# Keys and values of the memory: two heads to a pass, 512 columns wide, in two accumulators

## The chip, the cores and the metric

The kernel runs on one core of one Trainium2 chip. The time is the device time of one execution in microseconds (us). The program has five engines: TensorE (PE in the profile; its weight loads are PEld), VectorE (DVE), ScalarE (ACT), GpSimd (POOL) and SyncE (SP), which issues most transfers.

## What is computed

One layer of a streaming encoder on 512 tokens of width 1024: a mixer of three head groups (causal pooling, an RWKV-7 recurrence in chunks of 64 tokens, differential attention), a cross-attention of 4 heads into 256 memory tokens, and a gated MLP. The change concerns the keys and values of the memory:

```python
def memory_cross_attention(xn, memn, wq, wk, wv, wo, q_norm, k_norm):
    q = rms_normalize((xn @ wq).reshape(B, S, XA_HEADS, XA_HEAD)) * q_norm
    k = rms_normalize((memn @ wk).reshape(B, M, XA_HEADS, XA_HEAD)) * k_norm
    v = (memn @ wv).reshape(B, M, XA_HEADS, XA_HEAD)
    s = jnp.einsum('bshd,bmhd->bhsm', q, k) * (XA_HEAD ** -0.5)
    p = jax.nn.softmax(s, axis=-1)
    o = jnp.einsum('bhsm,bmhd->bshd', p, v).reshape(B, S, D_MODEL)
    return o @ wo
```

M is 256, XA_HEADS is 4, XA_HEAD is 256, and `wk` and `wv` are 1024 x 1024.

## The kernel before

Every large product is made of three matmuls (`mm3`, lines 331 to 333): each operand is split into a high and a low part, and high x high, high x low and low x high are added up in one accumulator. The helper has the same three lines for all products, so in the profile they are told apart by tiles and shapes. Weights come in units of 128 x 1024 values, each loaded in two halves of 512 columns. For each half SyncE issues a transfer, ScalarE makes the high part (`wh`, line 174) and VectorE the low part (`wl`, line 175). Five halves of each part have room.

The memory's keys and values depend on the memory alone. They are made while the mixer runs: `k_rows(h)` and `v_rows(h)` for the four heads are the eight "K" steps of the string `MIX`, in which each letter stands for a piece of work and which gives the order in which the pieces are recorded. A scheduler then orders the instructions of each engine. It may move work up to where its operands and buffers are ready, and it uses the K matmuls, which wait for nothing but weights, between pieces that wait.

One K step (`mgroup`, lines 995 to 1007) takes the 256 weight columns of one head. It makes 16 products (8 blocks of the contraction by 2 blocks of memory rows), that is 48 matmuls with 256 streaming columns. Both row blocks share one bank of PSUM, tag `a0`, which has one buffer; the last step uses a bank of tag `pd`. For K, ScalarE copies the bank out (line 1014). The step "k" (`k_norm`) sums squares, takes a power on GpSimd (line 1023) and scales on VectorE (line 1026). The step "e" (`k_t`) transposes on TensorE into a bank of tag `a0` (line 1034), and ScalarE copies that out (line 1037). The tags `a0`, `a1` and `b` also serve the large products of the mixer and of the output projection ("w"), and `pr` (two buffers) the recurrence and the scores of differential head 0.

Around the K steps stand these pieces. "t", "y" and "u" finish the inverse of the recurrence (`TX` line 805, `Y` line 814, `U` line 823). "a" makes `AT` (line 840). "c" is a chunk of the recurrence: `U` (line 905), a sum on VectorE (line 907), the state matmul `S` (line 916), and two more on VectorE (lines 923 and 924), from which the next chunk's `U` starts. "s", "o", "n" and "q" are the scores (`S`, lines 331 to 333, and VectorE's line 750), the outputs (`pT` line 775, `o`), the norm (`ss` line 788) and the transposes (`qkT` line 726) of differential attention. `k_norm` needs the rstd of the memory (line 402), which stands on GpSimd's queue behind four powers for the second pair of differential heads (line 680).

Of the kernel before, what the change touches and what calls it, by code (L numbers as in the profile page):

```python
# [10 lines left out]
F32 = mybir.dt.float32  # L11
F32R = mybir.dt.float32r
AF = mybir.ActivationFunctionType
# [3 lines left out]
P = 128  # L17
# [3 lines left out]
M = 256  # L21
# [50 lines left out]
def _pack(inputs):  # L72
    I = {k: np.asarray(v) for k, v in inputs.items()}
    f = {k: v[0] for k, v in I.items()}
    cols = []
    for n, w in _PCOLS:
        cols.append(f[n].reshape(w, P).T)
    pvec = np.concatenate(cols, 1)
    z64 = np.zeros((64, 64), np.float32)
    pw = f["pool_w"]  # L80
    pool = [np.block([[pw[2 * i], z64], [z64, pw[2 * i + 1]]]) for i in range(2)]
    wa2 = np.concatenate([f["rwkv_w2"], f["rwkv_a2"]], 0)
    lqk = np.concatenate([f["diff_lq1"], f["diff_lk1"], f["diff_lq2"], f["diff_lk2"]])
    pmat = np.concatenate(pool + [wa2, f["rwkv_g2"], np.tile(lqk[None], (P, 1))], 1)

    def fgroup(w, c0, ko):
        g = w[:, c0:c0 + 256].reshape(-1, P, 256)[list(ko)].transpose(1, 0, 2)
        return [g[:, 0:4].reshape(P, 1024), g[:, 4:8].reshape(P, 1024)]

    def tgroup(w):  # L90
        g = w.reshape(-1, P, 512).transpose(1, 0, 2)
        return [g[:, 2 * i:2 * i + 2].reshape(P, 1024) for i in range(g.shape[1] // 2)]

    def fpair(w, c0, c1, ko):
        a, b = fgroup(w, c0, ko), fgroup(w, c1, ko)
        return [a[0], b[0], a[1], b[1]]

    std = tuple(range(8))
    u = []
    wi = f["w_in"]  # L100
    for c0 in (1024, 256, 512, 768):
        u += fgroup(wi, c0, std)
    qk = [np.concatenate([wi[:, 1280 + c:1536 + c], wi[:, 1792 + c:2048 + c]], 1) for c in (0, 256)]
    one = lambda us: [[x] for x in us]
    kv = [fgroup(f[w], c0, std) for w in ("xa_wk", "xa_wv") for c0 in range(0, 1024, 256)]
    mix = {"A": one(tgroup(qk[0])), "V": one(tgroup(wi[:, 2304:2816])), "B": one(tgroup(qk[1])),
           "z": one(fgroup(wi, 0, std)),
           "K": kv,
           "w": one(fpair(f["w_out"], 0, 256, std) + fpair(f["w_out"], 512, 768, std))}
    for name in MIX:  # L110
        if name in mix:
            u += mix[name].pop(0)
    for w, ko in ((f["xa_wq"], std), (f["xa_wo"], std)):
        u += fpair(w, 0, 256, ko) + fpair(w, 512, 768, ko)
    for g in range(11):
        u += fpair(f["ffn_w_up"], g * 256, FF + g * 256, std)

    wd = f["ffn_w_down"].reshape(NF // 2, 2, P, 2, 512)
    wdown = np.stack([wd[:, 0, :, 0], wd[:, 0, :, 1], wd[:, 1, :, 1], wd[:, 1, :, 0]], 1)
    wpack = np.stack(u, 0)  # L120
    cst, bias = _consts()
    return {
        "xt": np.ascontiguousarray(I["x"][0].T),
        "memt": np.ascontiguousarray(I["mem"][0].T),
        "wp": np.ascontiguousarray(wpack),
        "wd": np.ascontiguousarray(wdown),
        "pvec": np.ascontiguousarray(pvec),
        "pmat": np.ascontiguousarray(pmat),
        "cst": cst,
        "bias": bias,  # L130
    }
# [15 lines left out]

MIX = ("iiiAAiiAAiiViVVVtjztqsyuzsjsyjsoajcBBoamconBpucjpmmBucmuccqKssccsgKsqkkososoKseogKkfsq1Ken"  # L150
       "ossoKfsKxensofooxfxxfk2fnefxwxfxwKwwwxwww1H2QQQQRSQST1RT2STSQQQRSOTOSTORO21TOSOTSTXOOXXXXX"
       "XXN")


# [39 lines left out]
def trunk_body(ctx: ExitStack, tc: tile.TileContext, A):  # L194
# [37 lines left out]
    def kvs(dt=F32, shape=(P, 512)):  # L232
        return slot("kv", TB["kv"], shape, dt)
# [10 lines left out]
    def pr(nm=None):  # L244
        return ps("pr", nm)

    def pd(nm=None):
        return ps("pd", nm)
# [517 lines left out]
    def diff_o(h, pair, keys):  # L766

        if h not in po:
            po[h] = pd("o") if h == 0 else ps("a1", "o") if h == 1 else pr("o")
        pt, m, cols = pd("pT"), 0, []  # L770
        for b in keys:
            qs = [i for i in pair if i >= b]
            cols.append((b, m, qs[0] * P, len(qs) * P))
            for i in qs:
                PE.transpose(pt[:, m:m + P], sc0[h, i][:, b * P:(b + 1) * P], ident)  # L775
                m += P
        ph, pl = pslot(), pslot()
        split(pt[:, 0:m], ph[:, 0:m], pl[:, 0:m])
        hs = slice(h * P, (h + 1) * P)
        for b, c, q0, n in cols:  # L780
            mm3(po[h][:, q0:q0 + n], vd[b][0][:, hs], vd[b][1][:, hs], ph[:, c:c + n], pl[:, c:c + n],
                b == 0, b == pair[1])
# [209 lines left out]
        ACT.activation(u, pt, AF.Copy, scale=pcol("pool_scale", i))  # L992
        ypl.append(u)

    def mgroup(tag="a0"):

        pt = ps(tag)
        for u in range(2):
            w = W.get(M)
            for j in range(4):  # L1000
                for t in range(2):
                    k = 4 * u + j
                    ah, al = mn[k]
                    sl = slice(t * P, (t + 1) * P)
                    mm3(pt[:, t * M:(t + 1) * M], ah[:, sl], al[:, sl], w[j][0], w[j][1],
                        k == 0 and t == 0, k == 7 and t == 1)
        return pt.rearrange("p (t m) -> p t m", t=2)

    KTr, Vr, kr = [], [], {}

    def k_rows(h):
        pt = mgroup()
        kr[h] = kvs(F32, (P, 2, M))
        ACT.activation(kr[h], pt, AF.Copy)

    def k_norm(h):
        k, kq = kr[h], kvs(F32, (P, 2, M))
        ss, r = small("kss", (P, 2)), small("kr", (P, 2))
        for t in range(2):
            ACT.activation(kq[:, t], k[:, t], AF.Square, accum_out=ss[:, t:t + 1])  # L1020
        V.tensor_tensor(ss, ss, rsm, ALU.mult)
        V.tensor_scalar(ss, ss, EPS, None, ALU.add)
        G.tensor_tensor(r, ss, mhalf[:, 0:2], ALU.pow)
        V.tensor_tensor(r, r, rm[0], ALU.mult)
        for t in range(2):
            V.tensor_scalar(k[:, t], k[:, t], r[:, t:t + 1], None, ALU.mult)

    def k_t(h):
        k = kr.pop(h)
        pt = ps("a0", "kT")  # L1030
        p4 = pt.rearrange("p (j m) -> p j m", j=2)
        for t in range(2):
            for j in range(2):
                PE.transpose(p4[:, j, t * P:(t + 1) * P], k[:, t, j * P:(j + 1) * P], ident)
        kt = xl(F32, (P, 2, M))
        for j in range(2):
            ACT.activation(kt[:, j], p4[:, j], AF.Copy, scale=pcol("xa_k_norm", j))
        KTr.append(kt)

    def v_rows(h):  # L1040
        pt = mgroup("pd" if h == H - 1 else "a0")
        v = xl(F32, (P, 2, M))
        for t in range(2):
            ACT.activation(v[:, t], pt[:, t], AF.Copy, scale=rm[0][:, t:t + 1])
        Vr.append(v)


    steps = {
# [427 lines left out]
```

## Time and profile before

| | us |
|---|---|
| median of 3 runs | 799.62 |
| lowest, highest | 798.34, 800.51 |
| the profiled execution's own time | 798.25 |
| its span, first to last instruction | 796.5 |
| TensorE busy in it | 785.5 |
| VectorE busy | 560.3 |
| ScalarE busy | 421.4 |

The rows are read as follows. Times count from the span's start. A matmul's row shows its whole length, in which the next one overlaps it; what TensorE pays for one is the distance to the next row's start. The granted clock is a share of 2.4 GHz, so 0.50 is 1.2 GHz. Where an engine stood idle, the row shows in brackets for how long and what ended it.

### The profile page before, as it was taken

The page shows a single profiled execution, that of the slowest core. Times are in us where ns is not written, and L with a number is a line of the kernel's source. Part 1 is how long each engine was busy: PE and PEld are TensorE (multiplying, and loading weights), DVE is VectorE, ACT ScalarE, POOL GpSimd, SP SyncE. Part 2 cuts the span into 40 slices and gives each one's busy share as a digit, 9 for nine tenths or more (in the row PEclk, how much of TensorE's full clock was granted, in tenths as well). Part 3 has the DMA queues.
Part 4 walks back from the last instruction along what each step waited for, and adds up shares of the span by engine and source line. Part 5 has one row for each costly group of instructions (what it writes and reads, how often), then busy time and mean ns, then how long its engine had stood idle before and what let it go on. Part 6 is the DMA issues. An engine that isn't in the chain of part 4 may idle for free.

```text
span 796.5 us, 11547 instructions
## 1 busy us (share of the span) xinstructions
PE 785.5 (99%) x4130; PEld 653.0 (82%) x4130; DVE 560.3 (70%) x1075; ACT 421.4 (53%) x778; POOL 64.2 (8%) x83
## 2 busy tenths in 40 slices
PE   9999999989899999999999999999999999999997
PEld 6867788879798888888888888888888888888886
DVE  7668668856898845656646577666666667898995
ACT  7464553575689854456545344433434344454662
POOL 4010400243500000000100000000000000000000
PEclk9999999979999999999999999999999999999999
DMA  7412114222031153221112322222232323534432
GB/s 278 135 56 95 64 54 133 88 74 91 16 107 55 69 168 135 94 93 54 40 66 80 133 92 93 92 94 92 93 105 81 106 94 133 176 114 133 132 93 79
DMA packets 43625, 79.22 MB, mean 99 GB/s; under 512 B 4784, under 2 KB 5936, under 8 KB 43568
## 3 DMA queue, kind: packets, MB, share of 16 engines
q1 hardware_dynamic: 41328, 75.35, 28.1%
q10 hardware_dynamic: 2240, 3.15, 1.2%
q8 instruction: 32, 0.52, 0.3%
q14 instruction: 25, 0.20, 0.1%
HBM read 76.38 MB, written 2.10 MB: 99 GB/s over the span
## 4 chain that ended last, share of the span: by engine, by line
PE 95%; ACT 1%; POOL 1%; DVE 1%; issue 1%; DMA 0%; DVEq 0%; SPq 0%; ACTq 0%
PE ps L331 23%; PE ps L333 22%; PE ps L332 22%; PE ps L1406 13%; POOL s_r L680 1%; PE T L575 1%; PE tr L523 1%; PE S L331 1%; PE colsum L393 1%; PE S L332 1%; PE S L333 1%; PE pT L775 1%; PE Sx L331 1%; PE W L608 1%; PE Sx L333 0%
## 5 line engine op out<-in xcount | busy, mean ns | idle before, releaser
L174 ACT ACTIVATE wh<-wr 128x512 fp32r<-128x512 f32 x212 | 132.5, 629 | 157.9 <-PE ps L332 119.7
L175 DVE TENSOR_TENSOR wl<-wr,wh 128x512 fp32r<-128x512 f32 x212 | 145.9, 690 | 99.5 <-ACT wh L174 95.2
L331 PE MATMUL ps<-r,wh 128*128 128x512 f32 x416 | 162.3, 394 | 0.0
L332 PE MATMUL ps<-r,wh 128*128 128x512 f32 x416 | 162.0, 389 | 0.0
L333 PE MATMUL ps<-r,wl 128*128 128x512 f32 x416 | 161.2, 390 | 0.0
L331 PEld LDWEIGHTS ps<-r,wh 128*128 128x128 f32 x416 | 78.1, 188 | 16.4 <-issue 0.2
L332 PEld LDWEIGHTS ps<-r,wh 128*128 128x128 f32 x416 | 78.1, 188 | 16.3 <-DVE t L762 0.2
L333 PEld LDWEIGHTS ps<-r,wl 128*128 128x128 f32 x416 | 78.1, 188 | 16.3
L1406 PE MATMUL ps<-whid,ma 128*128 128x512 f32 x276 | 85.2, 389 | 0.0
L331 PE MATMUL ps<-wh,xh 128*128 128x256 f32 (+1 forms) x224 | 75.3, 336 | 0.1
L332 PE MATMUL ps<-wl,xh 128*128 128x256 f32 (+1 forms) x224 | 74.8, 334 | 0.0
L1406 PEld LDWEIGHTS ps<-whid,ma 128*128 128x128 f32 x276 | 51.7, 188 | 11.2 <-ACT whid L312 0.5
L1406 PE MATMUL ps<-wlod,ma 128*128 128x512 f32 x138 | 53.4, 389 | 0.0
L312 ACT ACTIVATE whid<-r 128x512 fp32r<-128x512 f32 x55 | 34.4, 631 | 30.1 <-PE ps L1406 20.1
L1353 DVE TENSOR_TENSOR t<-ps,rb 128x512 f32<-128x512 f32 x44 | 29.4, 687 | 27.4 <-PE ps L333 27.0
L331 PEld LDWEIGHTS ps<-wh,xh 128*128 128x128 f32 x224 | 42.4, 189 | 5.4 <-issue 0.7
L332 PEld LDWEIGHTS ps<-wl,xh 128*128 128x128 f32 x224 | 42.4, 189 | 4.5 <-issue 0.7
L332 PE MATMUL ps<-xl,wh 128*128 128x512 f32 x112 | 44.0, 396 | 0.0
L313 DVE TENSOR_TENSOR wlod<-r,whid 128x512 fp32r<-128x512 f32 x55 | 37.2, 693 | 4.7 <-ACT whid L312 4.5
L332 PE MATMUL ps<-d,wh 128*128 128x512 f32 x96 | 37.7, 392 | 0.0
L333 PE MATMUL ps<-wh,xl 128*128 128x512 f32 x96 | 37.6, 393 | 0.0
L333 PE MATMUL ps<-d,wl 128*128 128x512 f32 x96 | 37.5, 390 | 0.0
(343 smaller groups left out, 1471.6 us busy)
## 6 DMA issues: line engine op xcount, KB each, us to landing
wr<-in_wp_dram SPq DMA_DIRECT2D x212, 256.0 KB, 2.6
r<-in_wd_dram SPq DMA_DIRECT2D x33, 256.0 KB, 2.8
wrawd<-in_wd_dram SPq DMA_DIRECT2D x22, 256.0 KB, 2.6
r<-in_xt_dram SPq DMA_DIRECT2D x8, 256.0 KB, 4.6
t<-in_xt_dram ACTq DMA_DIRECT2D x8, 256.0 KB, 2.7
out_dram<-t SPq DMA_DIRECT2D x8, 256.0 KB, 2.0
kv<-in_memt_dram ACTq DMA_DIRECT2D x4, 256.0 KB, 4.6
pm<-in_pmat_dram SPq DMA_DIRECT2D x1, 512.0 KB, 4.7
```

The source lines that it names most:

```text
L174: nc.scalar.activation(hi, raw, AF.Copy)
L175: nc.vector.tensor_tensor(lo, raw, hi.bitcast(F32), ALU.subtract)
L312: ins = ACT.activation(dhi, src, AF.Copy)
L313: V.tensor_tensor(dlo, src, dhi.bitcast(F32), ALU.subtract)
L331: mm(out, lh, rh, start=start, stop=False)
L332: mm(out, lh, rl, start=False, stop=False)
L333: mm(out, ll, rh, start=False, stop=stop)
L393: mm(pt[:, 2 * i:2 * i + 2], tot[:, i * P:(i + 1) * P], ones[:, 0:2], start=True, stop=True)
L523: PE.transpose(pv4[0:n, c, p, :], src(p, 2 * q + c), ident)
L575: mm(pts[hh].rearrange("p (c h t) -> p c h t", c=2, h=2)[:, c, p], KB[p][o:o + 64, cg, :], RA[p][o:o + 64, cg, :], start=True, stop=True)
L1353: V.tensor_tensor(dst[c], src[c], rb2, ALU.mult)
L1406: mm(X[p][tt], l, r, start=not onto and k == 0 and j == 0, stop=k == NG - 1 and j == 2, skip_group_check=onto)
```

## The change

A K step now takes half of the contraction for two heads at a time: 512 weight columns, two row blocks, each row block in a bank of its own (`a0` and `a1`; for the last pair of V two banks of `pd`). Two steps make one pair of heads, so the two banks are held from the first step to the end of the second. The weights are packed accordingly, four blocks of 128 x 512 in a step. There are again eight steps, each of 24 matmuls with 512 streaming columns. The copies out are as many as before and of the same sizes, and they come after every second step. The K tiles are now one per row block with two heads side by side, `k_norm` and `k_t` take their slices, and `k_t` uses `a0` for even and `a1` for odd heads. The output of differential head 1 moves from `a1` to a bank of `pr`. In `MIX` the steps K, k, e and some of their neighbours stand in another order.

```diff
-    kv = [fgroup(f[w], c0, std) for w in ("xa_wk", "xa_wv") for c0 in range(0, 1024, 256)]
+    kv = []
+    for w in ("xa_wk", "xa_wv"):
+        for c0 in (0, 512):
+            us = tgroup(f[w][:, c0:c0 + 512])
+            kv += [us[0:2], us[2:4]]
...
-MIX = ("iiiAAiiAAiiViVVVtjztqsyuzsjsyjsoajcBBoamconBpucjpmmBucmuccqKssccsgKsqkkososoKseogKkfsq1Ken"
-       "ossoKfsKxensofooxfxxfk2fnefxwxfxwKwwwxwww1H2QQQQRSQST1RT2STSQQQRSOTOSTORO21TOSOTSTXOOXXXXX"
+MIX = ("iiiAAiiAAiiViVVVtjztqsyuzsjsyjsoajcBBoamconBpucjpmmBucmuccqKKkkssccsgeesqosoKsoKsogkkfsq1e"
+       "eKnossoKfsxnsofooxfxx2KffnfxwxfxwKwwwxwww1H2QQQQRSQST1RT2STSQQQRSOTOSTORO21TOSOTSTXOOXXXXX"
...
-            po[h] = pd("o") if h == 0 else ps("a1", "o") if h == 1 else pr("o")
+            po[h] = pd("o") if h == 0 else pr("o")
...
-    def mgroup(tag="a0"):
-
-        pt = ps(tag)
+    mpt = []
+
+    def mgroup(i, tags):
+
+        if i % 2 == 0:
+            mpt[:] = [ps(t, "kv") for t in tags]
         for u in range(2):
-            w = W.get(M)
-            for j in range(4):
-                for t in range(2):
-                    k = 4 * u + j
-                    ah, al = mn[k]
-                    sl = slice(t * P, (t + 1) * P)
-                    mm3(pt[:, t * M:(t + 1) * M], ah[:, sl], al[:, sl], w[j][0], w[j][1],
-                        k == 0 and t == 0, k == 7 and t == 1)
-        return pt.rearrange("p (t m) -> p t m", t=2)
+            w = W.get(512)
+            last = i % 2 and u
+            for t, j in ([(t, j) for t in range(2) for j in range(2)] if last
+                         else [(t, j) for j in range(2) for t in range(2)]):
+                k = 4 * (i % 2) + 2 * u + j
+                ah, al = mn[k]
+                sl = slice(t * P, (t + 1) * P)
+                mm3(mpt[t], ah[:, sl], al[:, sl], w[j][0], w[j][1], k == 0, k == 7)
...
-    def k_rows(h):
-        pt = mgroup()
-        kr[h] = kvs(F32, (P, 2, M))
-        ACT.activation(kr[h], pt, AF.Copy)
+    def k_rows(i):
+        mgroup(i, ("a0", "a1"))
+        if i % 2:
+            kt = [kvs() for _ in range(2)]
+            for t in range(2):
+                ACT.activation(kt[t], mpt[t], AF.Copy)
+            for h in (i - 1, i):
+                kr[h] = [x[:, (h % 2) * M:(h % 2 + 1) * M] for x in kt]
...
-        pt = ps("a0", "kT")
+        pt = ps(("a0", "a1")[h % 2], "kT")
...
-    def v_rows(h):
-        pt = mgroup("pd" if h == H - 1 else "a0")
-        v = xl(F32, (P, 2, M))
-        for t in range(2):
-            ACT.activation(v[:, t], pt[:, t], AF.Copy, scale=rm[0][:, t:t + 1])
-        Vr.append(v)
+    def v_rows(i):
+        mgroup(i, ("a0", "a1") if i < 2 else ("pd", "pd"))
+        if i % 2:
+            v = [xl(F32, (P, 2, M)) for _ in range(2)]
+            for t in range(2):
+                for h in range(2):
+                    ACT.activation(v[h][:, t], mpt[t][:, h * M:(h + 1) * M], AF.Copy,
+                                   scale=rm[0][:, t:t + 1])
+            Vr.extend(v)
```

The diff shows little of what this does to the order. Three places on TensorE follow. In the names `ps` (before) and `kv` (after) are the accumulators of the K steps. Line numbers of the changed kernel are a few higher.

First place, the scores of differential head 0 (`S`) and the first `Y` of the inverse. Before:

```order
L331 MATMUL ps_2079<-wh_1_1798,xh_2020 128x256
L332 MATMUL ps_2079<-wl_1_1799,xh_2020 128x256
L333 MATMUL ps_2079<-wh_1_1798,xh_2021 128x256
L331 MATMUL S_1416<-d_1409,qz_866 128x128
L332 MATMUL S_1416<-d_1410,qz_866 128x128
L333 MATMUL S_1416<-d_1409,qz_867 128x128
L331 MATMUL S_1422<-d_1409,qz_868 128x128
L332 MATMUL S_1422<-d_1410,qz_868 128x128
L333 MATMUL S_1422<-d_1409,qz_869 128x128
L814 MATMUL Y_211_1434<-b_1182,b_1316 32x32 x16
L823 MATMUL U_212_1452<-kv_805,b_1182 64x64 x8
```

The same place after:

```order
L335 MATMUL S_1422<-d_1409,qz_868 128x128
L336 MATMUL S_1422<-d_1410,qz_868 128x128
L337 MATMUL S_1422<-d_1409,qz_869 128x128
L335 MATMUL kv_2079<-wh_1_2088,xh_2020 128x512
L335 MATMUL kv_2080<-wh_1_2088,xh_2020 128x512
L336 MATMUL kv_2079<-wl_1_2089,xh_2020 128x512
L337 MATMUL kv_2079<-wh_1_2088,xh_2021 128x512
L336 MATMUL kv_2080<-wl_1_2089,xh_2020 128x512
L337 MATMUL kv_2080<-wh_1_2088,xh_2021 128x512
L818 MATMUL Y_211_1434<-b_1182,b_1316 32x32 x16
L827 MATMUL U_212_1452<-kv_805,b_1182 64x64 x8
```

Both steps of the first pair, 48 matmuls of 512 columns, now stand ahead of `Y`, the last ten of them between and behind the two scores; before, one step stood there, and all of it ahead of the scores.

Second place, `AT` and what follows it; `o` is the output of differential head 0, `S_1637` the state matmul of chunk 0. Before, the end of a run of 18 K matmuls behind `AT`:

```order
L331 MATMUL ps_2272<-wh_1_1908,xh_1889 128x256
L332 MATMUL ps_2272<-wl_1_1909,xh_1889 128x256
L333 MATMUL ps_2272<-wh_1_1908,xh_1890 128x256
L916 MATMUL S_1637<-r_596,r_693 128x128
L331 MATMUL o_1592<-p_1597,d_1300 128x256
L916 MATMUL S_1637<-r_596,r_693 128x128
L331 MATMUL ps_2272<-wh_1_1908,xh_1889 128x256
L332 MATMUL ps_2272<-wl_1_1909,xh_1889 128x256
L332 MATMUL o_1592<-p_1598,d_1300 128x256
```

After:

```order
L844 MATMUL AT_1609<-b_1182,r_596 64x64 x8
L844 MATMUL AT_1609<-b_1182,r_597 64x64 x8
L335 MATMUL o_1592<-p_1597,d_1300 128x256
L920 MATMUL S_1637<-r_596,r_693 128x128 x2
L336 MATMUL o_1592<-p_1598,d_1300 128x256
L337 MATMUL o_1592<-p_1597,d_1301 128x256
L335 MATMUL o_1592<-p_1597,d_1304 128x128
L336 MATMUL o_1592<-p_1598,d_1304 128x128
L337 MATMUL o_1592<-p_1597,d_1305 128x128
L779 MATMUL pT_1717<-cs,t_1535 128x128
```

From here to the third place there were 96 K matmuls of 256 columns, and now there is none. `ss` of differential head 0, which stood ahead of the last `U` and `pool` before the state matmul of chunk 3, now stands just ahead of that state matmul.

Third place, the transposes of K (`kT`) and the next K step. Before, some way ahead of it:

```order
L905 MATMUL U_2049<-b_2036,at 128x128 x2
L1034 MATMUL kT_2590<-cs,kv_2152 128x128 x4
L331 MATMUL S_2237<-d_2075,qz_866 128x384
L332 MATMUL S_2237<-d_2076,qz_866 128x384
L333 MATMUL S_2237<-d_2075,qz_867 128x384
L331 MATMUL S_2243<-d_2075,qz_868 128x384
L332 MATMUL S_2243<-d_2076,qz_868 128x384
L333 MATMUL S_2243<-d_2075,qz_869 128x384
```

After:

```order
L909 MATMUL U_2245<-b_2036,at 128x128 x2
L1044 MATMUL kT_2321<-cs,kv_2177 128x128 x2
L1044 MATMUL kT_2321<-cs,kv_2178 128x128 x2
L1044 MATMUL kT_2329<-cs,kv_2177 128x128 x2
L1044 MATMUL kT_2329<-cs,kv_2178 128x128 x2
L920 MATMUL S_2251<-r_599,r_779 128x128 x2
L335 MATMUL kv_2427<-wh_0_2106,xh_1750 128x512
L336 MATMUL kv_2427<-wl_0_2107,xh_1750 128x512
```

Before, the transposes of one head came ahead of the fourth K step; now those of two heads, the scores up to 512 columns and one more chunk's `U` and `S` come ahead of the third.

## Rows read from the trace of the kernel before

**Rows 1.** The page: its head, the clock strip, the chain by engine.

```profile
span 796.5 us, 11547 instructions
...
PEclk9999999979999999999999999999999999999999
...
PE 95%; ACT 1%; POOL 1%; DVE 1%; issue 1%; DMA 0%; DVEq 0%; SPq 0%; ACTq 0%
```

**Rows 2.** Groups by shape, TensorE: count, busy us, mean ns.

```profile
L331 PE MATMUL ps<-wh,xh 128*128 128x256 f32 x128 | 37.6, 294 | 0.1
```

**Rows 3.** Timeline, TensorE: start us, length us, line, tiles, shape.

```profile
133.09 0.39 PE L331 MATMUL ps<-wh,xh 128*128 128x512 f32 x1
...
153.27 0.39 PE L333 MATMUL ps<-wh,xl 128*128 128x512 f32 x1
153.50 0.28 PE L331 MATMUL ps<-wh,xh 128*128 128x256 f32 x1
...
157.85 0.28 PE L333 MATMUL ps<-wh,xh 128*128 128x256 f32 x1
...
161.44 0.28 PE L333 MATMUL ps<-wh,xh 128*128 128x256 f32 x1
```

**Rows 4.** Windows: length; PE, PEld, DVE, ACT, POOL busy (count); granted clock; DMA share; GB/s.

```profile
161.00:166.40 5.40, 2.96 (x46) 2.46 (x44) 2.82 (x10) 4.87 (x11) 0.00 (x0) 1.00 0.20 69
166.40:176.60 10.20, 10.20 (x68) 8.86 (x69) 5.24 (x19) 5.57 (x14) 7.35 (x13) 0.50 0.15 51
178.00:201.30 23.30, 23.30 (x216) 21.17 (x214) 15.81 (x28) 15.33 (x35) 8.21 (x12) 1.00 0.23 79
207.60:212.20 4.60, 2.10 (x17) 1.70 (x15) 3.16 (x8) 2.36 (x4) 3.20 (x3) 1.00 0.00 0
217.70:300.00 82.30, 82.20 (x550) 73.16 (x551) 63.77 (x164) 64.01 (x146) 1.39 (x2) 1.00 0.29 97
```

**Rows 5.** Windows of tile `ps` alone: PE, PEld, DVE, ACT busy; then as above.

```profile
178.00:201.30 23.30, 13.46 (x96) 12.00 (x96) 0.00 (x0) 0.58 (x1) 1.00 0.23 79
```

**Rows 6.** Timeline, TensorE, with idle time ahead in brackets.

```profile
162.40 0.33 PE L331 MATMUL S<-d,qz 128*128 128x128 f32 x1 [0.68 <-ACT b L807]
...
164.47 1.19 PE L814 MATMUL Y<-b,b 32*32 32x32 f32 x32 [1.04 <-DVE s_nmx L750]
166.39 1.94 PE L823 MATMUL U<-kv,b 64*64 64x64 f32 x16 [0.72 <-issue]
...
176.92 1.15 PE L840 MATMUL AT<-b,r 64*64 64x64 f32 x32
...
184.81 0.71 PE L905 MATMUL U<-b,at 128*128 128x128 f32 x4
...
200.04 0.61 PE L905 MATMUL U<-b,at 128*128 128x128 f32 x4
...
201.35 0.61 PE L916 MATMUL S<-r,r 128*128 128x128 f32 x4
...
212.03 0.71 PE L916 MATMUL S<-r,r 128*128 128x128 f32 x4 [2.04 <-DVE r L907]
```

**Rows 7.** The chain that ended last, in order of time: start us, us, what.

```profile
197.05 1.07 PE ss L788 x2
...
209.70 1.11 POOL m_rstd L402
...
215.00 0.91 DVE kv L1026 x2
...
217.02 0.73 ACT xl L1037 x2
...
217.80 0.39 PE ps L331
```

**Rows 8.** Groups by line, 195 to 216 us on GpSimd, 176 to 220 us on VectorE.

```profile
L680 POOL TENSOR_TENSOR s_r<-s_ms,mhalf 128x8 f32<-128x8 f32 x4 | 8.2, 2088 | 2.1 <-DVE s_ms L678 2.1
...
L681 DVE SCALAR_TENSOR_TENSOR d<-d,x_rstd,s_r 128x512 f32<-128x512 f32 x4 | 3.3, 828 | 2.4 <-POOL s_r L680 2.4
```

More of the change, by code (lines that the diff above doesn't have):

```diff
@@ L1019, in k_norm @@
         for t in range(2):
-            ACT.activation(kq[:, t], k[:, t], AF.Square, accum_out=ss[:, t:t + 1])
+            ACT.activation(kq[:, t], k[t], AF.Square, accum_out=ss[:, t:t + 1])
         V.tensor_tensor(ss, ss, rsm, ALU.mult)
@@ L1025, in k_norm @@
         for t in range(2):
-            V.tensor_scalar(k[:, t], k[:, t], r[:, t:t + 1], None, ALU.mult)
+            V.tensor_scalar(k[t], k[t], r[:, t:t + 1], None, ALU.mult)
     def k_t(h):
         k = kr.pop(h)
-        pt = ps("a0", "kT")
+        pt = ps(("a0", "a1")[h % 2], "kT")
         p4 = pt.rearrange("p (j m) -> p j m", j=2)
@@ L1033, in k_t @@
             for j in range(2):
-                PE.transpose(p4[:, j, t * P:(t + 1) * P], k[:, t, j * P:(j + 1) * P], ident)
+                PE.transpose(p4[:, j, t * P:(t + 1) * P], k[t][:, j * P:(j + 1) * P], ident)
         kt = xl(F32, (P, 2, M))
```

## The prediction, made before the changed kernel was run

> **What bounds the kernel now.** I read four views in this order. First the page: the chain that ended last is 95% TensorE, over a span of 796.5 us, and the clock strip shows one slice of forty below 9 [rows 1]. So what counts is TensorE's own work, its few idle stretches, and its clock. Second, the groups by shape: the memory's keys and values are 384 matmuls of 256 columns, 128 on each of the three lines of the helper [rows 2]. Third, TensorE's timeline and the windows: between 161.4 and 166.4 us it stood idle three times (0.68, 1.04 and 0.72 us) [rows 6], and from 166.4 to 176.6 it was busy all 10.20 us at a granted clock of 0.50, the lower of its two levels [rows 4]. From 178.0 to 201.3 it was busy all the time at 1.00, but 96 of its matmuls there, two of the eight K and V steps, are of the form that this change replaces [rows 4, 5]: they fill the time in which the chunk chain of the recurrence and the attention heads hand work from engine to engine. From 207.6 to 212.2 it was busy only 2.10 of 4.60 us [rows 4]. Fourth, the chain across that hole: the `ss` matmul at 197.05, ScalarE, four powers on GpSimd (2088 ns each), the memory's rstd at 209.70, VectorE's scaling of K, and at 217.80 the next K group [rows 7, 8]. From 217.7 to 300 TensorE is busy 82.20 of 82.30 us [rows 4].
>
> **The matmuls.** The shape that K and V get (128 activation columns as weights, 512 weight columns streaming) is in the trace already: from 133.09 to 153.27 us lie 89 steps of it, 226.7 ns each. The 256-column form takes 30 steps from 157.85 to 161.44, 119.7 ns [rows 3]. So 384 x 119.7 = 45.96 us becomes 192 x 226.7 = 43.53 us: **-2.4 us**, or 0.30 us for each of the eight steps, which cost 5.74 us before and cost 5.44 now. Each is on the path, since TensorE ends last. The Trainium skill (TensorE: Matmul & The Clock Gate, Back-to-back issue gap) gives a matmul a fixed cost of about 2.5 ns beside its columns; by it the 192 fewer matmuls would be worth 0.5 us. The rows here say 12.7 ns (2 x 119.7 - 226.7), and the sum goes by them. The number of weight bytes, of their conversions and of the copies out of the accumulators is unchanged, and these lie beside TensorE.
>
> **What moves.** The order shows more than the shape. The first two steps, 48 matmuls, now all stand before the first `Y`. The next pair needs the same two accumulators, which the transposes of the first two heads take in between, so no K matmul stands between `Y` and those transposes, where 96 stood. I follow TensorE through four places, and count "ahead" as the earlier arrival less the K work that is still owed.
>
> *To `AT`.* From 153.50 to `Y` at 164.47 are 10.97 us: 5.74 of K, 1.72 of idle, 3.5 of the rest [rows 3, 6]. Now 10.88 of K cover that idle: `Y` at 153.5 + 10.88 + 3.5 = 167.9. With its 1.2 us and the same 0.72 us of hand-over, the work that took 10.20 us at 0.50 starts at 169.8. At the full clock it is 5.1 us, so `AT` lies between 174.9 and 180.0. The scores share two banks that VectorE must read first, so I take the middle, 177.4, against 176.92 [rows 6]. One more K step is done: ahead by 5.74 - 0.5 = **5.3 us** (2.7 to 7.8). A clock that stays up is the larger half of it.
>
> *To the state matmul `S` of chunk 3.* Before, 178.0 to 201.35; less 96 x 119.7 = 11.5 us of K and 0.9 us of `pool`, which now comes later, 10.9 us of TensorE's work are left [rows 5, 6]. Without a wait it would end at 178.5 + 10.9 = 189.4. But three turns of the chunk chain and the copies of `AT` lie bare now; with a turn of `U` about 7.6 us before (184.81 to 200.04, two turns) and half of that filler, I take 2 us of waits: 191.5 (189.4 to 194). Ahead by 201.35 - 191.5 - 5.44 - 0.9 = **3.5 us** (1.0 to 5.6).
>
> *To the next K step.* `ss` stands just ahead of that `S`, so at 190.6. From `ss` the chain took 217.80 - 197.05 = 20.75 us, 8.2 of them GpSimd's powers, with VectorE's queue held behind them for 2.4 us [rows 7, 8]. None of it gets shorter. It now ends with two heads' scalings, transposes and copies, 1.6 us more (0.91 us of scaling is in the rows for one). K starts again at 190.6 + 20.75 + 1.6 = 213.0. TensorE has done 2 us more by then (scores of 512 columns, a chunk turn, four transposes). Ahead by 217.8 - 213.0 - 5.44 + 2.0 = **1.4 us** (-0.6 to 3.5): two thirds of what the earlier stretch gave is lost in this stall, in which TensorE now idles some 5 us instead of 2.5.
>
> *The rest.* Five steps at 0.30 us: 1.5 us more, **2.9 us ahead** if nothing else happens. Two things do. (a) Some 9 us of work behind `S` of chunk 3, from about 200.4 to 203.8 by this count, TensorE has hardly anything to do. A hole like that preceded the fall to 0.50 at 166.4 (2.96 of 5.40 us busy), but 2.10 of 4.60 busy at 207.6 did not bring one [rows 4]. I charge 1.4 us (0 to 3.5: 7 us at half rate, at most). (b) The second pair ends in the same way: the next two heads' transposes need both accumulators, and ahead of the V steps stand some 9 us of scores, transposes and head outputs without filler. VectorE was busy for 63.77 of the 82.30 us from 217.7 on, so its queue sets their pace where nothing covers it [rows 4]. By the 2 us of waits on 10.9 us above I charge 1.8 us (0 to 4); before, that place was covered by 256-column K and V steps, and TensorE never waited. Sum: -2.9 + 1.4 + 1.8 = **+0.3 us**. The profiled execution took 798.25 us (span 796.5), so 798.6; the median of the runs shown, 799.62, is 1.4 us above it, so **799.9 us**.
>
> **Rivals.**
> *The clock and the cover hold (0.30).* If neither (a) nor (b) comes, -2.9 us; if fewer waits arise before chunk 3 too, up to -5: 794.5 to 797, likeliest 796.5. For it: 207.6 to 212.2 ran at 1.00 with less than half of it busy, and the front stretch no longer has its three gaps. Against: the chain from `ss` is the same.
> *The clock falls in the new bare stretch (0.29).* Behind `AT`, at about 178.6, TensorE waits for VectorE's copy of `U` and its own next operand, some 1.8 us with only small matmuls around it; the gaps before the fall at 166.4 were 1.04 and 0.72 us. If the clock goes to 0.50 there and no dense K stretch brings it back before 213, the 10.9 us of work up to chunk 3 take 21.8, less the waits of 2 us that they cover, and the whole GpSimd chain behind them shifts: up to +9, more likely +5, so 802 to 808, likeliest 804.5. It decides from the point where that wait is long enough to pull the clock down at all. For it: the same kind of small matmuls surrounded the first fall, and the 10 us that it lasted. The Trainium skill (TensorE: Matmul & The Clock Gate, A second HAM failure mode: psum-queue depth-cycling) says that short idles between groups of matmuls, when they come often, let the clock swing between its levels and cost throughput though a single matmul looks as fast as ever. The fall at 166.4 agrees, the stretch at 207.6 does not.
> *The skill's fixed cost of 2.5 ns (0.02).* Then 1.9 us of the 2.4 are missing: 801.8. Rows 3 speak against it.
> *That nothing of the sort is done* is out: the order of the changed kernel has 192 such matmuls.
>
> **How the numbers follow.** The forecast has 0.39, around 799.9, mostly within 797.3 to 802. 0.3% of the time, 2.4 us, is about what a measurement of this kernel can tell from no change. Faster by more than that: the first rival and the lower edge of the forecast, 0.32. Slower: the second rival and the upper edge, 0.31. Within: 0.37. The range leaves out about a tenth on either side: 795 to 805.5.
>
> **What would show it.** Right: 192 matmuls at 227 ns; no idle before `Y`; a granted clock near 1.00 from 166 to 178; no K matmul from `Y` to the first transposes of K; idle on TensorE of about 5 us in the stretch of the GpSimd powers; K again about 4.8 us earlier than before. Wrong: a clock of 0.50 for ten microseconds behind `AT` (slower), or TensorE busy through the powers (faster). If from the output projection on the two traces differ by more than 1 us in length, my view that nothing behind it moves is wrong.

## The result

The changed kernel takes 803.85 us (median of 5 runs, 803.53 to 806.3) against 798.88 us (5 runs, 798.34 to 800.51). The ratio is 1.0063, 95% interval 1.0047 to 1.0079: slower by 4 to 6 us. The forecast was 799.9; the result lies in its range, on the side that had 0.31.

The profiled execution has a span of 802.0 us, 5.5 more than before [rows 1]. The head of its page, the clock strip and the chain:

```profile
span 802.0 us, 11165 instructions
...
PEclk9999999998999999999999999999999999999999
...
PE 92%; ACT 4%; DVE 2%; DMA 1%; issue 1%; DVEq 0%; SPq 0%; ACTq 0%
```

The chain now leaves TensorE for 4% ScalarE and 2% VectorE (1% each before). To see where the time lies I cut both traces at the same two places: the first K matmul, and the first matmul of the cross-attention's queries (`ps<-d,wh`), which comes right behind the output projection. TensorE's timeline of the changed kernel:

```profile
155.41 0.39 PE L335 MATMUL kv<-wh,xh 128*128 128x512 f32 x1
...
169.43 1.19 PE L818 MATMUL Y<-b,b 32*32 32x32 f32 x32
172.66 1.11 PE L827 MATMUL U<-kv,b 64*64 64x64 f32 x16 [2.03 <-ACT b L819]
...
181.38 1.15 PE L844 MATMUL AT<-b,r 64*64 64x64 f32 x32 [0.79 <-DVE s_nmx L754]
...
185.48 0.71 PE L909 MATMUL U<-b,at 128*128 128x128 f32 x4 [0.27 <-ACT at L846]
187.59 0.55 PE L779 MATMUL pT<-cs,t 128*128 128x128 f32 x3 [1.40 <-DVE t L766]
...
198.98 0.61 PE L920 MATMUL S<-r,r 128*128 128x128 f32 x4
...
214.77 0.44 PE L335 MATMUL S<-d,qz 128*128 128x384 f32 x1 [0.94 <-DVE s_nmx L754]
...
218.07 0.50 PE L335 MATMUL kv<-wh,xh 128*128 128x512 f32 x1
...
329.80 0.39 PE L335 MATMUL ps<-d,wh 128*128 128x512 f32 x1
```

The second marker of the kernel before:

```profile
324.23 0.39 PE L331 MATMUL ps<-d,wh 128*128 128x512 f32 x1
```

So there are three parts. Up to the first K matmul: 155.41 against 153.50 [rows 3], 1.9 us more, although TensorE's order is the same up to there; in the 14 profiles of this study that start lies between 153.5 and 155.4, whatever the kernel (the last section says what it is). Between the markers: 174.4 against 170.7 us, **3.7 us more**. Behind them: 472.2 against 472.3. The change's own cost is the 3.7 us, and I call that stretch the interval.

Windows of the changed kernel (length; TensorE busy, count; granted clock; DMA share; GB/s). The first answers to the window with the fall of the clock before, the next two are the two falls that replace it [rows 4]:

```profile
166.40:176.60 10.20, 8.15 (x77) 0.90 0.53 179
174.80:178.00 3.20, 3.20 (x24) 0.50 0.09 29
188.40:195.00 6.60, 6.33 (x35) 0.50 0.00 0
```

ScalarE's timeline shows what the 2.03 us in front of `U` are. The copy of `Y` (L819) stands behind three conversions of weights (L178) for the second pair of keys, the first of which waited for its transfer; before, TensorE stood 0.72 us in front of that `U` [rows 6]:

```profile
169.33 0.63 ACT L178 ACTIVATE wh<-wr 128x512 fp32r<-128x512 f32 x1 [2.12 <-DMA wr<-in_wp_dram]
...
171.33 0.61 ACT L178 ACTIVATE wh<-wr 128x512 fp32r<-128x512 f32 x1
171.97 0.59 ACT L819 ACTIVATE b<-Y 32x512 f32<-32x512 f32 x1
```

### The profile page after: what moved, and what is told of

Same layout as the page of the kernel before. It is cut to its first block, busy times and chain, and to the rows that moved or that the text cites. A ratio compares the mean times of both kernels' runs of the same rounds, so it can differ in the third digit from the quotient of the medians.

```text
span 802.0 us, 11165 instructions
## 1 busy us (share of the span) xinstructions
PE 786.9 (98%) x3938; PEld 644.5 (80%) x3938; DVE 559.8 (70%) x1075; ACT 422.3 (53%) x778; POOL 60.6 (8%) x83
## 4 chain that ended last, share of the span: by engine, by line
PE 92%; ACT 4%; DVE 2%; DMA 1%; issue 1%; DVEq 0%; SPq 0%; ACTq 0%
PE ps L335 21%; PE ps L336 20%; PE ps L337 20%; PE ps L1419 13%; PE kv L335 1%; PE kv L336 1%; PE kv L337 1%; ACT t L332 1%; PE colsum L397 1%; PE T L579 1%; PE tr L527 1%; ACT wh L178 1%; PE U L827 1%; DMA wr<-in_wp_dram 1%; PE Sx L335 1%
## 5 line engine op out<-in xcount | busy, mean ns | idle before, releaser
L179 DVE TENSOR_TENSOR wl<-wr,wh 128x512 fp32r<-128x512 f32 x212 | 146.1, 692 | 103.0 <-ACT wh L178 98.7
L178 ACT ACTIVATE wh<-wr 128x512 fp32r<-128x512 f32 x212 | 132.2, 628 | 159.7 <-PE ps L336 120.6
L336 PE MATMUL ps<-wl,xh 128*128 128x512 f32 x96 | 38.2, 398 | 0.0
L335 PE MATMUL ps<-wh,xh 128*128 128x512 f32 x96 | 37.7, 393 | 0.0
L336 PE MATMUL ps<-d,wh 128*128 128x512 f32 x96 | 37.7, 392 | 0.0
L335 PE MATMUL ps<-d,wh 128*128 128x512 f32 x96 | 35.4, 392 | 0.0
L335 PE MATMUL ps<-xh,wh 128*128 128x512 f32 x80 | 31.6, 408 | 0.7 <-ACT xh L319 0.7
```

The lines of the kernel that those rows point to most:

```text
L178: nc.scalar.activation(hi, raw, AF.Copy)
L179: nc.vector.tensor_tensor(lo, raw, hi.bitcast(F32), ALU.subtract)
L335: mm(out, lh, rh, start=start, stop=False)
L336: mm(out, lh, rl, start=False, stop=False)
```

## The account of the interval

For every kernel I added up TensorE's rows of the interval. Each row is paid the distance to the next row's start less the idle time in brackets. Of that, what a window of one microsecond lost by its granted clock (paid time times one less the clock) goes into "low clock", the remainder to K/V matmuls or to all other matmuls. The four columns add up to the interval, to 0.1. How a row is divided where the clock changes within it moves up to 0.6 us between "low clock" and "others".

| kernel | median us | ratio to before, 95% | interval | idle | low clock | K/V | others |
|---|---|---|---|---|---|---|---|
| before | 798.9 to 800.1 | 1 | 170.7 | 4.9 | 5.1 | 49.5 | 111.2 |
| changed | 803.85 | 1.0047 to 1.0079 | 174.4 | 8.7 | 5.2 | 45.7 | 114.8 |
| e3: changed, narrow matmuls | 802.83 | 1.0024 to 1.0050 | 174.9 | 7.2 | 3.1 | 48.7 | 116.0 |
| e4: before, head 1 in `pr` | 803.36 | 1.0030 to 1.0066 | 175.0 | 7.4 | 4.6 | 49.2 | 113.8 |
| e2: before, letters changed | 805.62 | 1.0053 to 1.0098 | 179.0 | 9.7 | 7.7 | 48.5 | 113.2 |
| f1: before, seventh K late | 799.74 | 0.9979 to 1.0004 | 171.2 | 6.3 | 2.9 | 48.7 | 113.3 |
| h_k: keys wide only | 801.97 | 1.0012 to 1.0035 | 174.2 | 6.9 | 7.2 | 47.8 | 112.3 |
| h_v: values wide only | 808.27 | 1.0085 to 1.0117 | 179.6 | 9.8 | 7.7 | 47.8 | 114.3 |
| c1: second pair's keys first | 804.66 | 1.0046 to 1.0083 | 177.0 | 10.1 | 2.8 | 45.8 | 118.2 |
| c7: c1, half a pair behind `Y` | 805.81 | 1.0070 to 1.0104 | 176.7 | 8.9 | 3.3 | 45.7 | 118.8 |
| d1: last values early | 808.47 | 1.0057 to 1.0127 | 180.7 | 11.3 | 9.8 | 45.6 | 114.0 |
| g1: c1 and d1 | 808.15 | 1.0062 to 1.0125 | 177.5 | 10.9 | 4.6 | 45.9 | 116.2 |
| g2: c7 and d1 | 808.50 | 1.0075 to 1.0131 | 179.6 | 10.2 | 6.7 | 46.0 | 116.7 |
| e5: `Y`'s copy ahead | 813.89 | 1.0119 to 1.0211 | 184.4 | 10.3 | 14.7 | 46.0 | 113.4 |

The interval is from one profiled execution each, the median from 4 to 10 runs, which differ by up to 4 us within a kernel (9 in e5); differences of a microsecond in either column decide nothing. Profiles differ by more than that even where TensorE's order is the same. In d1 that order is the changed kernel's up to 107.5 us of the interval, and d1 comes to the same place 2.9 us later: its fall of the clock behind `AT` lasts 13.7 us instead of 6.6 (d1's row stands below). h_k has the changed kernel's order up to 90.8 us and comes there 1.1 us later. So the medians carry the verdicts, and one interval against another tells a place only where more than some 3 us are at stake. Behind the interval all 14 profiles have 472.2 or 472.3 us.

In the changed kernel the K/V matmuls cost 3.8 us less than before, and the low clock costs the same. Idle time costs 3.8 us more and the other matmuls 3.6 us more. These others are equal in number and shape. A turn of the chunk's `U` shows one way in which such a row gets dearer. Before, a K matmul followed it, and four `U` matmuls were paid 0.47 us (184.81 to 185.28, [rows 6] and the row below). In the changed kernel TensorE stood idle behind them, and their whole length was paid, 0.71 us (185.48 above). Over the interval the 28 `U` matmuls of the chunks cost 0.7 us more, and the 48 output matmuls of 256 columns 0.7. How much of the 3.6 us has this reason in all is not shown. The kernel before:

```profile
185.28 0.36 PE L331 MATMUL ps<-wh,xh 128*128 128x256 f32 x1
```

## The experiments

### First, the forecast's own reasons: bare stretches

Theory 1: TensorE lacks K matmuls from `Y` to `kT`. Theory 2: the conversions that held `Y`'s copy.

**c1.** The transposes of the first two heads (`ee`) are recorded behind the second pair's K steps.

```diff
-...qKKkkssccsgeesqosoKsoKsogkkfsq1ee...
+...qKKkkssccsgsqosoKsoKeesogkkfsq1ee...
```

> The changed kernel with one edit: the transposes of the first pair's keys (e e) are recorded behind the second pair's K steps, so that the two accumulators go to the second pair's 48 K matmuls before they go to kT. Theory 1 (TensorE ran bare because the second pair could not start): between the first AT and kT there are K matmuls again; of the changed kernel's idle time from 181 to 218 us (0.79 + 0.27 + 1.40 + 0.27 + 0.25 + 0.34 + 0.59 + 0.94 = 4.9 us) some 3 to 4 us go, and so does the second stretch at clock 0.50 (188.4 to 195.0, worth 3.3 us); the 2.0 us in front of U and the first stretch at 0.50 stay. Time 797 to 799.5 us, against 803.9 of the changed kernel. Theory 2 (the weight conversions ahead of Y's copy on ScalarE are the cause): their order at that place is the same, so the time stays at 802 to 804 us, and the clock falls again behind AT.

Measured: 804.66 us, where theory 1 had 797 to 799.5. The stretch was filled. From 181 to 218 us TensorE was busy 34.63 of 37 us, and its clock was 0.95; in the changed kernel it was 32.41 and 0.91. First c1, then the changed kernel:

```profile
181.00:218.00 37.00, 34.63 (x272) 0.95 0.18 58
```

```profile
181.00:218.00 37.00, 32.41 (x272) 0.91 0.01 2
```

The loss by low clock fell from 5.2 to 2.8 us, but the interval grew by 2.6 us. The clock still fell behind `AT`, for 3.4 us instead of 6.6, as this window of c1 shows:

```profile
184.70:188.10 3.40, 3.16 (x10) 0.50 0.00 0
```

The first `kT` came 7 us later in the interval (68.0 against 61.1) with 48 more K matmuls done (10.9 us), so some 4 us were won up to there. Behind it, where those 48 were now missing, idle time and short matmuls took back more than that. Theory 2 named the fall and, nearly, the time (802 to 804); e5 takes its reason away.

**c7.** As c1, and the second half of the first pair waits for the first 16 `Y` matmuls.

```diff
+                if i == 1:
+                    with tc.issue_after(ymm[15]):
+                        mm3(mpt[t], ah[:, sl], al[:, sl], w[j][0], w[j][1], k == 0, k == 7)
...
```

> As the run with the second pair's keys first, and the second half of the first pair's K matmuls (24 of 48) is in addition ordered behind the first 16 Y matmuls, so that they can fill the wait between Y and U. Theory 1: Y starts 3 us earlier than in the changed kernel, the 2.0 us in front of U are covered, neither stretch at clock 0.50 appears (in the kernel before one cost 4.9 us), and the time is 792 to 796 us, faster than both. Theory 2: Y's copy still stands behind conversions, which the K matmuls now hide: 797 to 800 us. If the clock falls all the same, 797 to 799 us.

Measured: 805.81 us, above both theories. `Y` started 10.6 us behind the first K matmul instead of 14.0, as meant, and no wait stood in front of `U`; one of 1.68 us stood ahead of `Y` instead, in front of the scores. `AT` came no earlier (27.3 against 26.0 us), since the matmuls moved there now stood in front of it.

**e5.** ScalarE's conversions for the second key pair are ordered behind its copy of the first `Y`.

```diff
+            if self.late[0] <= i < self.late[1]:
+                with self.tc.issue_after(self.ycopy[0]):
+                    nc.scalar.activation(hi, raw, AF.Copy)
...
```

> The changed kernel with one edit: ScalarE's conversions of the second key pair's weights are ordered behind its copy of the first Y. Theory 2 (conversions that waited for their transfers held Y's copy): U starts at most 0.8 us after Y's last matmul instead of 2.0, the clock does not fall at 174.8 us (1.6 us less), and the time falls by about 3 us or more, to 799.5 to 801 us. Theory 1 (no K matmuls behind Y): the wait in front of U shrinks by its 1.3 us but the stretch from Y to kT has still no K matmuls, so at least 3 us of the other idle time and one long stretch at clock 0.50 remain: 801.5 to 804 us.

Measured: 813.89 us, 10 above the changed kernel. The wait did what theory 2 asked (0.51 us in front of `U`), and the time that it promised (799.5 to 801) did not come. Behind that, short matmuls and small waits followed, and from 174 to 200 us the clock stood at its lower level while TensorE was nearly always busy. First the timeline:

```profile
170.54 1.11 PE L835 MATMUL U<-kv,b 64*64 64x64 f32 x16 [0.51 <-ACT b L827]
...
172.73 0.40 PE L341 MATMUL S<-d,qz 128*128 128x256 f32 x1 [0.53 <-DVE s_nmx L760]
```

The window:

```profile
174.00:200.00 26.00, 24.74 (x182) 0.50 0.12 37
```

That is the loss which the forecast's second rival feared, at its longest, although it began 7 us ahead of `AT` (181.07 us here): 14.7 us lost by low clock, 9.5 more than in the changed kernel. The edit also moved later instructions, so 10 us is not the price of the wait alone, and what the wait was worth in the changed kernel stays open.

### Second: is it the lumps?

Theory 3: two banks lock the K work into lumps, and what stands at the end is missing earlier. Theory 4: a chain of scores and recurrence on other engines sets the pace, and K matmuls in between only delay it.

**d1.** The last pair of V in `a0` and `a1`, recorded among the scores of head 3.

```diff
-        mgroup(i, ("a0", "a1") if i < 2 else ("pd", "pd"))
+        mgroup(i, ("a0", "a1"))
...
-...eeKnossoKfsxnsofooxfxx2KffnfxwxfxwKwwwx...
+...eeKnossoKfsKxnsofoKoxfxx2ffnfxwxfxwwwwx...
```

> The changed kernel with its last pair of V in the accumulators a0 and a1 instead of two banks of pd, and recorded among the scores of head 3 instead of behind them, so that its 48 matmuls (10.9 us) stand ahead of the output projection. The interval from the first K matmul to the first matmul of the cross-attention's queries was 170.7 us before and 174.4 us in the changed kernel. Theory 3 (the K work comes in lumps that two banks lock; what is locked at the end is missing as filler earlier): the interval falls by 1 to 3 us, 801 to 803 us. Theory 4 (a chain of scores and recurrence on VectorE and ScalarE sets the end of the mixer, and K matmuls between only delay it): no gain, 804 to 807 us.

**g1** is c1 with d1, **g2** is c7 with d1.

> The run with the second pair's keys first (interval 177.0 us, with 5.6 us of idle time between 200 and 290 us) and the last V pair early as in the other run of this group. Theory 3: the last pair fills that idle time, the interval falls by 4 to 6 us to 171 to 173 us, and the time is 797 to 800 us. Theory 4: the idle time is that of the chain, whose steps come later by what is put between; 803 to 806 us.

> As the run before in this group, and the second half of the first key pair (24 matmuls) behind the first 16 Y matmuls. Theory 3: no bare stretch is left, 795 to 799 us, faster than or equal to the kernel before. Theory 4: as the other, 803 to 806 us.

Measured: 808.47, 808.15 and 808.50 us, slower than either theory had them. Part of the reason stands in g1's trace. The last K matmuls had covered the way from the last head's norm to the last feature of the output projection. With them gone, TensorE stands idle there. The longer of these two waits, 3.3 us, is in all three runs, the shorter in g1 and g2, and neither is in the changed kernel:

```profile
300.07 1.12 PE L790 MATMUL ss<-t,cs 128*128 128x512 f32 x2 [0.69 <-ACT t L788]
304.46 2.07 PE L333 MATMUL ps<-r,wh 128*128 128x512 f32 x4 [3.27 <-ACT r L314]
```

In d1's profile 2.9 of the 6.3 us over the changed kernel's interval arose ahead of its edit, by the longer fall of the clock named above. Its window:

```profile
182.60:196.30 13.70, 13.35 (x87) 0.50 0.00 0
```

**f1.** The kernel before, with its seventh K step where the changed kernel has its own.

```diff
-...KenossoKfsKxensofooxfxxfk2fnefxw...
+...KenossoKfsxensofooxfxxfk2Kfnefxw...
```

> The kernel before with one letter moved: the seventh of its eight K steps (head 2's V, 48 matmuls of 119.7 ns, 5.7 us) stands where the changed kernel has its seventh, behind the scores of head 3. Theory 3: 5.7 us of filler is missing earlier and stands at the end, 1.5 to 5 us slower than before, 800.5 to 804 us, without any change of width or banks. Theory 4: within 1 us of before, 798.5 to 800 us.

Measured: 799.74 us against 800.07; no difference. Theory 3 falls here too. Of theory 4 it stands that the K matmuls are filler everywhere and that moving them moves the waits. That a single chain sets the end is not shown: c1 to g2 changed that chain's own order as well.

### Third: one part of the change at a time

Theory 5: the move of head 1's output into `pr`. Theory 6: the pairing of the keys. Theory 7: that of the values.

**e4.** The kernel before with that move alone.

```diff
-            po[h] = pd("o") if h == 0 else ps("a1", "o") if h == 1 else pr("o")
+            po[h] = pd("o") if h == 0 else pr("o")
```

> The kernel before with one edit: the output of differential head 1 in a bank of pr instead of a1, as the changed kernel has it. The banks of pr are also those of the recurrence's U, S, y and of its norm; with the edit head 1's output matmuls stand behind the recurrence's gate on TensorE instead of in the midst of its chunks. Theory 5 (this move holds head 1 up and with it the chain of heads to the end of the mixer): 2 to 5 us slower, 801.5 to 804.5 us. Theories 6 and 7 (key pairs or value pairs cost the time): 798.5 to 800.5 us.

Measured: 803.36 us, 3.4 more than before in the same group, as theory 5 had it. The banks of `pr` serve the recurrence, its norm and its gate in the recorded order. Head 1's first output stood at 226.50 us before and now came behind the first gate. TensorE's timeline, first the rows of the kernel before, then those of e4:

```profile
226.50 0.37 PE L331 MATMUL o<-p,d 128*128 128x256 f32 x1
...
252.21 1.02 PE L788 MATMUL ss<-t,cs 128*128 128x512 f32 x2
```

```profile
251.32 1.02 PE L959 MATMUL gate<-r,pm 128*128 128x512 f32 x2
...
252.77 0.28 PE L331 MATMUL o<-p,d 128*128 128x256 f32 x1
...
262.50 1.07 PE L788 MATMUL ss<-t,cs 128*128 128x512 f32 x2
```

The last of these rows is head 1's norm (`ss`). Before, it stood at 252.21, here some 10 us later, 9.5 of them within the interval. The last `ss` was 4.3 us later within it, and so was the end.

**e2.** The kernel before with the changed kernel's letters and nothing else.

```diff
-...qKssccsgKsqkkososoKseogKkfsq1KenossoKfsKxensofooxfxxfk2fnefxwxfxwKwww...
+...qKKkkssccsgeesqosoKsoKsogkkfsq1eeKnossoKfsxnsofooxfxx2KffnfxwxfxwKwww...
```

> The kernel before (256 columns, one head to a K step, one accumulator) with nothing but the letters of the changed kernel's order table. There the fourth K step comes behind the first kT, the third still ahead of it. Theory 1: half of the filler is missing behind AT, so 0.5 to 3 us slower than before, 799.5 to 802 us, and K matmuls are missing from about 190 us to kT. Theory 2: Y's copy stands as before, so 798.5 to 799.5 us. If the wide form as such cost the time, this run would equal before too.

Measured: 805.62 us, 6 more, where theory 1 had 0.5 to 3. So the letters cost even more where nothing else is changed. By f1 the late seventh step among them costs nothing by itself. The letters were written for two accumulators and meet one here, so the 6 us need not be what they cost in the changed kernel.

**h_k and h_v.** Only the keys, or only the values, in wide pairs; the other half as in the kernel before. Both have head 1 in `pr`.

```diff
 h_k (from the changed kernel)
+    kv += [fgroup(f["xa_wv"], c0, std) for c0 in range(0, 1024, 256)]
-...eeKnossoKfsxnsofooxfxx2KffnfxwxfxwKwww...
+...eeKnossoKfsKxnsofooxfxx2ffnfxwxfxwKwww...
 h_v (from the kernel before)
+    kv = [fgroup(f["xa_wk"], c0, std) for c0 in range(0, 1024, 256)]
-...seogKkfsq1KenossoKfsKxensofooxfxxfk2fnefxw...
+...seogKkfsq1eKnossoKfsxensofooxfxxfk2Kfnefxw...
```

> The changed kernel with its keys as they are (two heads, 512 columns, letters up to the fourth e) and its values as in the kernel before (one head, 256 columns, one bank, letters as before from there). Theory 6 (the pairing of the keys, whose second pair must wait for kT, costs the time): as slow as the changed kernel or slower by the narrow values' 1.9 us, 803 to 807 us. Theory 7 (the pairing of the values): 797 to 800 us. Theory 5: 801 to 805 us.

> The kernel before with its keys as they are and its values in pairs of heads with 512 columns, the output of head 1 in pr, and the first pair's letters behind kT of head 1. Theory 6: the first part up to kT is that of the kernel before, and 96 wide matmuls save 1.9 us: 796.5 to 799 us. Theory 7: 801 to 805 us. Theory 5: 800 to 803 us.

Measured: 801.97 and 808.27 us. Theory 6 falls, in both runs: the keys' pairs, bare stretch included, are the milder half. Of the ranges only theory 5's for h_k holds; h_v is slower than all three. In h_v TensorE does up to `kT` what it did before (`kT` at 61.9 us of the interval, 62.2 before), and all of the 8.9 us is lost behind it. Of those 8.9, e4 has 4.3 by head 1 alone. If that carries over, the rest belongs to the paired values, their letters, or both.

**e3.** The changed kernel with each 512-column matmul issued as two of 256 columns into the same bank.

```diff
-                mm3(mpt[t], ah[:, sl], al[:, sl], w[j][0], w[j][1], k == 0, k == 7)
+                for n in (slice(0, M), slice(M, 2 * M)):
+                    mm3(mpt[t][:, n], ah[:, sl], al[:, sl], w[j][0][:, n], w[j][1][:, n],
+                        k == 0 and n.start == 0, k == 7 and n.start == M)
```

> The changed kernel with each 512-column K matmul issued as two of 256 columns into the two halves of the same bank: pairs, banks and letters stay, and only the width goes back (384 matmuls again). If the width is worth what its matmuls show (2.4 us by their pitch in runs, up to 3.9 us as they stand in the whole stretch), 806 to 808 us against 803.9. If a chain on other engines sets the time and hides the matmuls, 803.5 to 805 us.

Measured: 802.83 us, below both ranges, a microsecond below the changed kernel, and an interval 0.5 us above it: no difference that these runs can tell. In the account its K/V matmuls cost 3.0 us more, the others 1.2 more, and idle time and low clock cost 1.5 and 2.1 less. The median shows that the width is not worth its length here. That the idle time took it up is one reading of two profiles; the 2.1 us of clock are no more than profiles of one order differ by. The clock fell behind `AT` in e3 too, about as long as in the changed kernel:

```profile
184.90:191.70 6.80, 6.53 (x36) 0.50 0.01 2
```

## Where the prediction held and where it failed

The range held the result; the count that led to its middle did not hold. Place by place, against the forecast, TensorE fell behind by 2.1 us up to `AT` and by 3.5 more up to the state matmul, gained 2.4 up to the next K step, and lost 0.2 behind it: 3.4 us in all, for +3.7 where +0.3 stood.

**The matmuls.** Right. There are 192, at the distance forecast, 227 ns:

```profile
218.41 0.39 PE L336 MATMUL kv<-wl,xh 128*128 128x512 f32 x1
218.63 0.39 PE L337 MATMUL kv<-wh,xh 128*128 128x512 f32 x1
218.86 0.39 PE L335 MATMUL kv<-wh,xh 128*128 128x512 f32 x1
```

Against before, the K/V matmuls cost 3.8 us less in place, against e3 3.0; forecast were 2.4. The 3.0 us are 16 ns for each of the 192 matmuls saved. The Trainium skill's fixed cost of about 2.5 ns (TensorE: Matmul & The Clock Gate, Back-to-back issue gap) does not agree, as rows 3 had said. What failed is the sentence behind it, that each of them "is on the path, since TensorE ends last". TensorE did end last, but these matmuls stand where it would otherwise wait. e3 shows what that means for the time: with the width taken back, nothing is lost.

**To `AT`.** Forecast 5.3 us ahead. On the interval's own time `AT` came at 26.0 us against 23.4, with one K step more done: 5.74 - 2.55 = 3.2 ahead. No idle time stood in front of `Y`, as forecast; it came at 14.0 us (forecast 14.4), and the long fall of the clock at 166.4 was gone. What went wrong lies behind `Y`. The 0.72 us of hand-over became 2.03 behind the weight conversions. My text said that the conversions "lie beside TensorE"; they stood ahead of `Y`'s copy on ScalarE. From `U` to `AT` it took 8.7 us, where the middle that I took had 7.6. The clock fell there for 3.2 us, so the sign of a clock near 1.00 up to 178 failed, but that cost 1.6 us where my middle held 2.5. A wait of 0.79 us ahead of `AT` and dearer rows, for which I had charged nothing, cost more than this saved.

**To `S` of chunk 3.** This is the step that failed most. It gives 201.35 - 153.50 = 47.9 us against 198.98 - 155.41 = 43.6; less 5.44 us of K and 0.9 of `pool`, that is 2.1 us behind, where 3.5 ahead were forecast. I had charged 2 us of waits, and there were 2.2 (0.27 + 1.40 + 0.27 + 0.25). On top came the 6.6 us at 0.50 from 188.4 on, 3.2 us lost. That is the second rival's mechanism, in the stretch that it named, some eight microseconds later than it said. It is no accident of one profile. In the three profiles with this order up to there (changed, h_k, d1), and in e3, the clock fell 29 to 33 us behind the first K matmul, for 6.6 to 13.7 us. In the five with the order of the kernel before (before, e2, e4, f1, h_v) it stood at 1.00 from 29 to 36 us. The clock was the right suspect for that stretch.

**To the next K step.** 218.07 - 155.41 = 62.7 against 64.3 us, so 1.8 us behind, 1.4 ahead forecast. The 5 us of idle time in the stretch of GpSimd's powers did not come: waits of 0.34, 0.59 and 0.94 us stood there. From `ss` to the K step it took 20.05 us (198.02 to 218.07), where 22.35 were forecast. "None of it gets shorter", my text said of that chain, but the four powers took 6.46 us instead of 8.2 [rows 8]. GpSimd's row in the changed kernel:

```profile
201.99 6.46 POOL L684 TENSOR_TENSOR s_r<-s_ms,mhalf 128x8 f32<-128x8 f32 x4 [0.71 <-DVE s_ms L682]
```

They took 6.5 us in e3, h_k and d1 too, and 8.2 in e4, f1 and h_v. Why the order should change them is not shown.

**The rest.** The same reckoning gives 3.7 - 1.8 = 1.9 us lost from there to the second marker. Forecast were 1.5 won, and 1.4 and 1.8 charged for (a) and (b), 1.7 lost. That sum held, and so did the behaviour behind the output projection: 472.2 and 472.3 us.

**The second rival's time.** It gave 804.5, and 803.85 came, but not by its sum, so the nearness is luck. The loss by low clock over the whole interval is 5.2 us, and it was 5.1 before. The fall behind `AT` took the place of the fall at 166.4. In c1 that fall lasted half as long, and c1 ended no earlier. So the trace names the place of a loss, and in c1 mending that place did not mend the time.

**What I didn't price.** I treated the order's other edits as carriers of the width. e4 and e2 show that either of them, put alone into the kernel before, costs time of the size of the whole change's 5 us: 3.4 and 6 us. The forecast has no term for head 1's bank; the diff showed that line.

**What stays open.** How the loss divides in the changed kernel itself. There the gate comes earlier (83.2 us of the interval against 95.9), and head 1's `ss` stands where it stood before (98.8 and 98.7), so e4's 4.3 us can't simply be carried over. Head 1's output in another bank of the changed kernel was not run, and the letters of the kernel before can't be put under wide pairs, since they place a `kT` between the two halves of a pair that holds both banks. No kernel here beat the kernel before.

## What to carry to other kernels

Matmuls that a scheduler uses as filler need not be worth their length. Here they were made shorter (against e3) or moved to where a gap was (c1, c7), and the time did not fall. So price them by what would be bare without them. Before an accumulator is moved to make room, see which other work shares the new bank's queue; in e4 one output in the recurrence's banks stood 25 us behind its old place, and the kernel was 3.4 us slower. Where a trace gives a place to a loss, mend that place alone before believing that it is the cause.

## Not expected of the hardware

The start. The first matmuls on real data, up to 10.4 us, stood 430 ns apart in the changed kernel's profile, nearly twice the 227 ns of the same shape elsewhere, as at the lower of the two levels; yet the granted clock of that window reads 1.00. In the kernel before the distance was 230 ns from 6.5 us on. The changed kernel, a window (all five engines' busy time, granted clock, DMA share, GB/s) and TensorE's timeline:

```profile
0.00:10.00 10.00, 8.02 (x18) 4.44 (x19) 4.24 (x7) 5.94 (x9) 4.55 (x19) 1.00 0.79 262
```

```profile
7.02 0.63 PE L337 MATMUL ps<-xh,wl 128*128 128x512 f32 x1
7.45 0.63 PE L336 MATMUL ps<-xl,wh 128*128 128x512 f32 x1
...
10.43 0.53 PE L337 MATMUL ps<-xh,wl 128*128 128x512 f32 x1
```

Before:

```profile
6.74 0.39 PE L332 MATMUL ps<-xl,wh 128*128 128x512 f32 x1
6.97 0.40 PE L333 MATMUL ps<-xh,wl 128*128 128x512 f32 x1
```

This is where the changed kernel's first K matmul got its 1.9 us. It isn't the change's: TensorE's order up to there is the same in all 14 profiles, and d1 and h_k, which share the changed kernel's order far beyond it, start their K matmuls at 153.67 and 153.83 us. Two profiles are better compared from a marker behind the start.

And the clock stayed low under load. In e5 it was at 0.50 for 26 us in which TensorE was busy 24.74, mostly with short matmuls. The same order of TensorE's instructions had the clock back after 6.6 us in the changed kernel's profile and after 13.7 us in d1's, in which it was busy for 13.35.
